# Two-layer trunk of GLA and dilated attention: the gate's columns side by side, heads two by two, another order in the first seven steps

## The chip, the cores and the metric

The kernel runs on one core of one Trainium2 chip. The metric is the device time of one execution in microseconds (us); the median of three runs stands for a kernel. TensorE (PE) multiplies, VectorE (DVE), ScalarE (ACT) and GpSimd (POOL) do the work on elements, SyncE (SP) issues most transfers.

## The reference

Batch 1, 256 positions, width 2048, two layers, all in float32:

```python
# layer 0: h = rmsnorm(x, norm_mix_g[0])
a_b, a_c, a_x, q, k, v, r, g_low = jnp.split(h @ w_in, IN_OFFSETS, axis=-1)
y_conv = a_b * causal_short_conv(a_c * a_x, conv_w)          # 1024 channels, width 3
log_a = jax.nn.log_sigmoid(g_low @ w_gate2 + b_gate) / 16.0  # g_low: rank 16, out: 512
o = gla_chunked(q, k, v, log_a)                              # 4 heads, dk 128, dv 256
o = rmsnorm(o, gla_norm_g) * jax.nn.silu(r)
x = x + concatenate([y_conv, o]) @ w_out
x = x + squared_relu_mlp(rmsnorm(x, norm_mlp_g[0]), w1, w2)  # 2048 -> 8192 -> 2048
# layer 1: 16 heads of 128; three dilated groups, ALiBi, merged by their denominators
x = x + dilated_attention(rmsnorm(x, norm_mix_g[1]), w_qkv, w_o)
x = x + squared_relu_mlp(rmsnorm(x, norm_mlp_g[1]), w1, w2)
return rmsnorm(x, final_norm_g)
```

## The kernel before

**Layout.** Activations lie transposed: 16 tiles of 128 features by 256 positions. Each product with a weight is made of three fp32r products: the weight and the activation are both split into a high and a low half (`split_high` by an ACT copy L124, `split_low` by a DVE subtraction L130; `scale_split` L203 and L204 do it for x, giving one tile xs of 512 columns, high 256 and low 256), and high x high, high x low and low x high are added up in PSUM (`three`, L133 is the line of every such product).

**Steps.** The weights come as 770 blocks of 128 x 1024, one to a step: a transfer by SP into one of four `raw` buffers, the two splits (four steps ahead), and 24 products of 256 columns (groups of kind "a", tile acc) or 12 of 512 columns (kind "b", tile accv, which gives v with positions on the partitions). Eight steps make a group; behind its last step the PSUM banks are read (`evac_...`). Step 0 to 7 give q and k of the first GLA pair. Steps 8 and 9 are the gate (kind "g", tile accg): its 16 columns filled up with zeros to 128, 48 products of 256 columns. Steps 10 to 17 give v, and from step 18 on r, the second pair, the convolution, w_out, the MLP, attention (per quad one v group and two groups of q and k), w_o and the second MLP follow.

**Sub-steps and background work.** A step has four sub-steps. In each, the main loop issues the products, in the second one also `split_low` four steps ahead and the next load, then what the group's end asks for (`g.evac`), and at its end calls `advance()`, which lets exactly one waiting generator go on by one piece:

```python
for item in bg:
    if item[1] <= clock[0]:        # due, in the order of the list
        wait = next(item[0], None)
        ...
        return
```

A generator says by `yield n` after how many sub-steps its next piece is due. Each engine executes in the order of issue, so this order is the order in every queue. In the background run: the sum of squares for the first norm (squares of tiles 0 to 11 on POOL, 12 to 15 on ACT and DVE), `norm_factor` (pss: sums over partitions, at sub-step 32; prb: the factor spread over partitions, 40; `R["b"]`, 41), the pieces that wait for `R["b"]` (`after_norm`: q, k, the gate), `gates()` (pz L367: the gate's second product; la L371 to L376: log sigmoid by Abs, Exp, Ln on ACT and one DVE piece), and `gla_pair` (pg L389: cumulative sums of la, then eight levels of scores). What starts them:

```python
spawn(first_norm(), 16)
spawn(after_norm(rest), 2)      # evac_glow; rest ends with spawn(gates(), 12)
triggers[len(steps)] = lambda pair=pair: spawn(gla_pair(pair), 6)   # behind the v group
```

`evac_v` copies each half of v from PSUM on ACT (L350) in the second and the fourth sub-step of the v group's last step.

**Attention.** `evac_aqk` writes q and k of a pair of heads on DVE and starts two generators `head(h)`, due 4 and 5 sub-steps later: bias and scores (pqk L584, L585), softmax, transposes (ppt L603), a copy (pT L606), the products with v (pao), and the split into y.

Of the kernel before, what the change touches and what calls it, by code (L numbers as in the profile page):

```python
# [49 lines left out]
def trunk_kernel(ctx: ExitStack, tc, xin, vecs, w_in, w_gate, w_gate2, w_out, w_qkv, w_o, w1, w2, w2f,  # L50
# [27 lines left out]

    gpool = tc.alloc_tile_pool(name="gla", bufs=1)
    msk = gpool.tile([P, 8, P], U8, name="msk")  # L80
    wg2 = gpool.tile([P, 512], F32, name="wg2")
    ap_ = {}

    def end_gla():

# [10 lines left out]

    busy = tmp.tile([P, T], F32, tag="sqp", bufs=1, name="busy")
    pool.memset(busy, 0.0)
    p = bank("warm")
    for _ in range(WARM):  # L100
        pe.matmul(p[:, :T], lhsT=busy[:, :P], rhs=busy, start=True, stop=True)
# [12 lines left out]

    def load(s):
        g, i = steps[s]
        raws[s] = wts.tile([P, 1024], F32, tag="raw", bufs=RAW, name=f"raw{s}")
        for c in parts(s):
            nc.sync.dma_start(raws[s][:, c], g.src[g.first + i, :, c])

    def split_high(s):
        his[s] = wts.tile([P, 1024], F32R, tag="wh", bufs=WB, name=f"wh{s}")
        for c in parts(s):
            act.activation(his[s][:, c], raws[s][:, c], AF.Copy)  # L124

    def split_low(s):
        r = raws.pop(s)
        los[s] = wts.tile([P, 1024], F32R, tag="wl", bufs=WB, name=f"wl{s}")
        for c in parts(s):
            dve.tensor_tensor(los[s][:, c], r[:, c], his[s][:, c].bitcast(F32), op=OP.subtract)  # L130
# [11 lines left out]
    def part_of(g, j):  # L142
        return g.ps[j // 2][:, (j % 2) * T:(j % 2 + 1) * T]

    def sub_a(g, i, j, wh, wl):
        if j // 2 not in g.ps:
            g.ps[j // 2] = bank(f"acc{j // 2}")
        p = part_of(g, j)
        for kk in range(2):
            n = 2 * i + kk  # L150
            c = slice(kk * 512 + j * P, kk * 512 + (j + 1) * P)

            three(p, wh[:, c], wl[:, c], g.rhs(n), n == 0 and j % 2 == 0, n == 15)
# [14 lines left out]
    def sub_g(g, i, j, wh, wl):  # L168
        if 0 not in g.ps:
            g.ps[0] = bank("accg")  # L170
        p = g.ps[0]
        for kk in range(2 * j, 2 * j + 2):
            n = 8 * i + kk
            c = slice(kk * P, (kk + 1) * P)
            three(p[:, :T], wh[:, c], wl[:, c], g.rhs(n), n == 0, n == 15)

# [137 lines left out]
        return ys[k]  # L316


    gl = {"ended": 0}

    def evac_qk(pair):
        def f(j, p):
# [28 lines left out]
        return f  # L351

    def evac_glow(j, p):
        t = grab(p, "sq", 2)
        ga = gl["ga"] = gpool.tile([32, T], F32, tag="ga", bufs=1, name="ga")
        dve.memset(ga, 1.0)

        def rest():
            dve.tensor_tensor(ga[:16, :], t[:16, :], R["b"][:16, :], op=OP.mult)
            spawn(gates(), 12)  # L360
        spawn(after_norm(rest), 2)

    def gates():
        la = gl["la"] = gpool.tile([P, 2, 512], F32, tag="la", bufs=1, name="la")
        ps = [bank("pz") for _ in range(2)]
        for tt in range(2):
            pe.matmul(ps[tt], lhsT=gl["ga"][:17, tt * P:(tt + 1) * P], rhs=wg2[:17, :],  # L367
                      start=True, stop=True)
        yield 3
        for tt in range(2):  # L370
            act.activation(la[:, tt, :], ps[tt], AF.Abs)  # L371
        act.activation(la, la, AF.Exp, scale=-1.0)
        act.activation(la, la, AF.Ln, bias=1.0)
        yield 1
        for tt in range(2):
            dve.scalar_tensor_tensor(la[:, tt, :], ps[tt], 0.0, la[:, tt, :], op0=OP.min,  # L376
                                     op1=OP.subtract)
        yield 1
# [186 lines left out]
    def evac_aqk(pair):  # L565
        def f(j, p):
            if j == 0:
                at["q", pair] = ap_["p"].tile([P, 2, T], F32, tag="gq", name="aq")
                at["k", pair] = ap_["p"].tile([P, 2, T], F32, tag="gk", name="ak")
            dst = at["q" if j < 2 else "k", pair][:, j % 2, :]  # L570
            dve.tensor_tensor(dst, p, R["b"], op=OP.mult)
            if j == 3:
                (spawn(head(2 * pair), 4), spawn(head(2 * pair + 1), 5))
        return f

    def head(h):
        q, k = at["q", h // 2][:, h % 2, :], at["k", h // 2][:, h % 2, :]
        v = at["v"][h // 4]
        vc = slice((h % 4) * DH, (h % 4 + 1) * DH)
        slope = 2.0 ** (-8.0 * (h + 1) / HEADS)  # L580
        bias = ap_["p"].tile([P, 384], F32, tag="bias", name="bias")
        dve.scalar_tensor_tensor(bias, ap_["dl"][:, 0, :], slope, ap_["dl"][:, 1, :], op0=OP.mult, op1=OP.add)
        ps = bank("pqk")
        pe.matmul(ps[:, :P], lhsT=q[:, :P], rhs=k[:, :P], start=True, stop=True)  # L584
        pe.matmul(ps[:, P:384], lhsT=q[:, P:], rhs=k, start=True, stop=True)  # L585
        yield 1
        st = ap_["p"].tile([P, 3, P], F32, tag="st", name="st")
        sf = st.rearrange("p b t -> p (b t)")
        dve.scalar_tensor_tensor(sf, ps[:, :384], DH ** -0.5, bias, op0=OP.mult, op1=OP.add)
        nm = ap_["p"].tile([P, 3], F32, tag="nm", name="nm")  # L590
        dve.tensor_reduce(nm, st, axis=AX.X, op=OP.max, negate=True)
        dve.tensor_tensor(nm[:, 1:2], nm[:, 1:2], nm[:, 2:3], op=OP.min)
        z = ap_["p"].tile([P, 2], F32, tag="z", name="z")
        act.activation(sf[:, :P], sf[:, :P], AF.Exp, bias=nm[:, 0:1], accum_out=z[:, 0:1])
        act.activation(sf[:, P:], sf[:, P:], AF.Exp, bias=nm[:, 1:2], accum_out=z[:, 1:2])
        yield 2
        dve.reciprocal(z, z)
        dve.tensor_scalar(sf[:, :P], sf[:, :P], z[:, 0:1], None, op0=OP.mult)
        dve.tensor_scalar(sf[:, P:], sf[:, P:], z[:, 1:2], None, op0=OP.mult)
        yield 9  # L600
        pt = bank("ppt")
        for b in range(3):
            pe.transpose(pt[:, b * P:(b + 1) * P], st[:, b, :], ident)  # L603
        yield 1
        pT = ap_["p"].tile([P, 384], F32, tag="pT", name="pT")
        act.activation(pT, pt[:, :384], AF.Copy)  # L606
        yield 3
        po = bank("pao")
        mm(po[:, :T], v[:, 0, vc], pT[:, :T], True, False)
        mm(po[:, P:T], v[:, 1, vc], pT[:, T:], False, True)  # L610
        yield 1
        y = y_tile(h)
        split_into(y, po[:, :T])
        yield 1


    hs = {}
# [40 lines left out]
    for pair in range(2):  # L658
        add(Group(w_in, 32 * pair, 8, "a", X, evac_qk(pair)))
        if pair == 0:  # L660
            add(Group(w_gate, 0, 2, "g", X, evac_glow))
        add(Group(w_in, 32 * pair + 8, 8, "b", X, evac_v(gl["v"], pair)))
        triggers[len(steps)] = lambda pair=pair: spawn(gla_pair(pair), 6)
        if pair == 0:
            add(Group(w_in, 16, 8, "a", X, evac_r(0)))
            add(Group(w_in, 24, 8, "a", X, evac_r(1)))
# [34 lines left out]
        load_x(s + 4)  # L701
        load(s + RAW)
    act.dma_start(cm, cmat)
    act.dma_start(wg2[:17, :], w_gate2)

    def first_norm():
        for k in range(12, NK):
# [13 lines left out]
            yield 8  # L721
    spawn(load_masks(), 40)

    SUB = {"a": (sub_a, 4), "b": (sub_b, 4), "g": (sub_g, 4)}
    for s, (g, i) in enumerate(steps):
        if s in triggers:
            flush()
            triggers[s]()
        if s < 4:
            first_scale(s + 4)  # L730
        if s + LA < len(steps):
            split_high(s + LA)
        f, n = SUB[g.kind]
        wh, wl = his.pop(s), los.pop(s)
        for j in range(n):
            f(g, i, j, wh, wl)
            if j == 1:
                if s + LA < len(steps):
                    split_low(s + LA)
                if s + LA + RAW < len(steps):  # L740
                    load(s + LA + RAW)
            flush()
            if i == g.n - 1:
                if g.kind == "a" and j % 2 == 1:
                    g.evac(j - 1, part_of(g, j - 1))
                    g.evac(j, part_of(g, j))
                    del g.ps[j // 2]
                elif g.kind == "b" and j % 2 == 1:
                    g.evac(j // 2, g.ps.pop(j // 2))
                elif g.kind == "g" and j == n - 1:  # L750
                    g.evac(0, g.ps.pop(0)[:, :T])
            advance()
    flush()
    while bg:
# [38 lines left out]
def _layout(x, norm_mix_g, norm_mlp_g, final_norm_g, hyb_w_in, conv_w, gla_w_gate2, gla_b_gate,  # L793
# [16 lines left out]
        c = slice(h * 512, h * 512 + 512)  # L810
        parts += [ac[:, c], ax[:, c], ab[:, c]]
    a["w_in"] = _blocks(np.concatenate(parts, axis=1))
    gp = np.zeros((2, P, 8, P), np.float32)
    gp[..., :16] = g.reshape(2, 8, P, 16).transpose(0, 2, 1, 3)
    a["w_gate"] = gp.reshape(2, P, 1024)
    a["w_gate2"] = np.concatenate([f(gla_w_gate2[0]), f(gla_b_gate[0])[None]], axis=0)
    wo = f(hyb_w_out[0]).reshape(NK, P, D)
    a["w_out"] = _blocks(wo[[0, 1, 2, 3, 8, 9, 10, 11, 12, 13, 14, 15, 4, 5, 6, 7]].reshape(D, D))
# [36 lines left out]
```

## Time and profile before

| | |
|---|---|
| median of three runs | 2186.46 us (2186.12 to 2186.83) |
| the profiled execution | 2186.37 us, its span 2184.2 us |
| PE, PEld (weight load) busy | 2168.6 us, 2137.3 us |
| DVE, ACT, POOL busy | 1323.4, 1038.8, 66.9 us |
| HBM read | 406.94 MB, 187 GB/s over the span |
| chain that ended last | PE 98%, DVE 1%, DMA 1% |

Matmuls are pipelined, and a busy PE is not PE at its peak. A product of 256 columns has a record of 276 ns, and the next one starts 0.11 us after it. The chain of waits is followed back from the last instruction, at each step to what released it.

### The profile page before, as it was taken

The numbers are of one execution on the slowest core, as the hardware profiler recorded it, in microseconds if no ns is written. First come the engines' busy times: TensorE is split into PE (matmuls) and PEld (weight loads), VectorE is DVE, ScalarE is ACT, GpSimd is POOL, SyncE is SP. The second block draws the span as 40 slices with busy tenths as digits, with TensorE's granted clock in tenths as the row PEclk, the third lists the DMA queues.
The fourth block names the chain that finished last, engine by engine and source line by source line (L and its number), as shares of the span: only waits on it lengthen the run. The fifth ranks groups of instructions, "written<-read, shape, count | busy, mean of one in ns | idle before, by whom it ended". The sixth has DMA issues, their size and how long they took to land.

```text
span 2184.2 us, 43375 instructions
## 1 busy us (share of the span) xinstructions
PE 2168.6 (99%) x18390; PEld 2137.3 (98%) x18390; DVE 1323.4 (61%) x1809; ACT 1038.8 (48%) x1414; POOL 66.9 (3%) x70
## 2 busy tenths in 40 slices
PE   9999999999999999999999999999999999999997
PEld 8999999999999999999999999999999999999997
DVE  7666766655556555656665655666555555555555
ACT  5555545444444354345444444545434534444553
POOL 4000230000000000000000000000000000000000
PEclk9999999999999999999999999999999999999999
DMA  7555566656666656665665555565666565666663
GB/s 264 159 171 166 163 201 186 196 190 208 186 199 189 202 184 203 190 198 183 205 191 169 177 176 174 173 195 186 199 194 194 189 198 191 197 195 195 191 199 117
DMA packets 114405, 411.86 MB, mean 189 GB/s; under 512 B 12817, under 2 KB 13201, under 8 KB 114210
## 3 DMA queue, kind: packets, MB, share of 16 engines
q1 hardware_dynamic: 113760, 408.47, 59.3%
q8 instruction: 144, 2.36, 0.4%
q10 hardware_dynamic: 450, 0.61, 0.1%
q14 instruction: 51, 0.42, 0.1%
HBM read 406.94 MB, written 2.10 MB: 187 GB/s over the span
## 4 chain that ended last, share of the span: by engine, by line
PE 98%; DVE 1%; DMA 1%; issue 0%; ACT 0%; SPq 0%; DVEq 0%; ACTq 0%
PE acc L133 88%; PE accv L133 6%; PE accg L133 1%; PE psc L450 1%; DMA raw<-w_in 1%; PE pao L133 0%; DVE wl L130 0%; PE pqk L585 0%; PE po L133 0%; PE ppt L603 0%; DVE xs L204 0%; DVE xf L761 0%; PE pqk L584 0%; PE pos L133 0%; PE pss L133 0%
## 5 line engine op out<-in xcount | busy, mean ns | idle before, releaser
L130 DVE TENSOR_TENSOR wl<-raw,wh 128x1024 fp32r<-128x1024 f32 (+1 forms) x771 | 936.7, 1229 | 708.0 <-ACT wh L124 707.3
L124 ACT ACTIVATE wh<-raw 128x1024 fp32r<-128x1024 f32 (+1 forms) x771 | 810.3, 1058 | 851.7 <-PE acc L133 739.5
L133 PE MATMUL acc<-xs,wh 128*128 128x256 f32 x6400 | 1100.8, 277 | 0.1
L133 PEld LDWEIGHTS acc<-xs,wh 128*128 128x128 f32 x6400 | 966.0, 188 | 1.7 <-ACT wh L124 0.8
L133 PE MATMUL acc<-xs,wl 128*128 128x256 f32 x3200 | 885.1, 277 | 2.2 <-DVE wl L130 2.2
L133 PE MATMUL acc<-hs,wh 128*128 128x256 f32 x3968 | 675.0, 276 | 0.0
L133 PEld LDWEIGHTS acc<-xs,wl 128*128 128x128 f32 x3200 | 600.9, 188 | 3.9 <-DVE wl L130 3.9
L133 PEld LDWEIGHTS acc<-hs,wh 128*128 128x128 f32 x3968 | 597.2, 188 | 0.0
L133 PE MATMUL acc<-hs,wl 128*128 128x256 f32 x1984 | 547.6, 276 | 0.0
L133 PEld LDWEIGHTS acc<-hs,wl 128*128 128x128 f32 x1984 | 372.4, 188 | 0.0
L133 PE MATMUL acc<-ys,wh 128*128 128x256 f32 x1024 | 175.3, 277 | 0.0
L133 PEld LDWEIGHTS acc<-ys,wh 128*128 128x128 f32 x1024 | 154.4, 188 | 0.1
L133 PE MATMUL acc<-ys,wl 128*128 128x256 f32 x512 | 141.4, 276 | 0.0
L133 PE MATMUL accv<-wh,xs 128*128 128x512 f32 x384 | 122.1, 399 | 0.0
L276 DVE TENSOR_TENSOR hs<-u,hs 128x256 fp32r<-128x256 f32 x128 | 54.5, 426 | 79.0 <-ACT hs L275 79.0
L133 PEld LDWEIGHTS acc<-ys,wl 128*128 128x128 f32 x512 | 96.1, 188 | 0.0
L275 ACT ACTIVATE hs<-u 128x256 fp32r<-128x256 f32 x128 | 53.4, 417 | 71.1 <-DVE u L627 71.1
L133 PEld LDWEIGHTS accv<-wh,xs 128*128 128x128 f32 x384 | 70.2, 188 | 14.3 <-issue 0.8
L133 PE MATMUL accv<-wl,xs 128*128 128x512 f32 x192 | 75.5, 393 | 0.0
L289 DVE TENSOR_TENSOR x<-x,t 128x256 f32<-128x256 f32 x128 | 54.4, 425 | 4.4
L627 DVE TENSOR_TENSOR u<-u 128x256 f32<-128x256 f32 x128 | 53.5, 418 | 0.0
L287 DVE TENSOR_TENSOR t<-acc,rb 128x256 f32<-128x256 f32 x124 | 51.8, 417 | 0.0
(148 smaller groups left out, 790.5 us busy)
## 6 DMA issues: line engine op xcount, KB each, us to landing
raw<-w SPq DMA_DIRECT2D x504, 512.0 KB, 4.3
raw<-w_qkv SPq DMA_DIRECT2D x96, 512.0 KB, 3.6
raw<-w_in SPq DMA_DIRECT2D x95, 512.0 KB, 3.7
raw<-w_out SPq DMA_DIRECT2D x32, 512.0 KB, 4.2
raw<-w_o SPq DMA_DIRECT2D x32, 512.0 KB, 4.3
raw<-w2f SPq DMA_DIRECT2D x8, 512.0 KB, 4.3
x<-xin SPq DMA_DIRECT2D x8, 256.0 KB, 5.9
out_dram<-xf SPq DMA_DIRECT2D x7, 256.0 KB, 2.3
```

The source lines that it names most:

```text
L124: act.activation(his[s][:, c], raws[s][:, c], AF.Copy)
L130: dve.tensor_tensor(los[s][:, c], r[:, c], his[s][:, c].bitcast(F32), op=OP.subtract)
L133: pe.matmul(out_, lhsT=lhsT, rhs=rhs, start=start, stop=stop, skip_group_check=True)
L275: act.activation(t[:, :T], v, AF.Copy)
L276: dve.tensor_tensor(t[:, T:], v, t[:, :T].bitcast(F32), op=OP.subtract)
L287: dve.tensor_tensor(t, p, R["b2"], op=OP.mult)
L289: dve.tensor_tensor(x[:, k, :], x[:, k, :], p, op=OP.add)
L450: pe.matmul(p[:, (2 * h + tt) * P:(2 * h + tt + 1) * P], lhsT=l[:, h, c], rhs=r[:, h, c], start=True, stop=True)
L627: dve.tensor_tensor(u, u, u, op=OP.mult)
```

## The change

Three edits. (1) In steps 0 to 6 `sub_a` calls `early`, which issues the products of the high weights for all four column blocks in the first two sub-steps and those of the low weights in the last two. (2) The gate becomes one step of kind "h": its weights come as one block of 128 x 256; ACT copies the high halves into columns 0 to 15 and DVE the low halves into columns 32 to 47 of four tiles wg3, which POOL has set to zero at the start. 16 products of 512 columns (xs high and low side by side) follow; `evac_glow` adds the two halves of the high rows, and the low rows stay apart until the second product, for which wg2 holds the gate's second matrix twice (49 rows, the last one the bias). (3) One generator `heads(pair)` does two heads at a time.

```diff
+    pool.memset(wg2[:32, :], 0.0)
+    wg3 = [const.tile([P, 4, P], F32R, tag=f"ys{4 + i}", name=f"wg3{i}") for i in range(4)]
+    for t in wg3:
+        pool.memset(t.bitcast(F32), 0.0)
...
     def split_high(s):
+        if steps[s][0].kind == "h":
+            r = raws[s][:, :256].rearrange("p (k c) -> p k c", c=16)
+            for q in range(4):
+                act.activation(wg3[q][:, :, :16], r[:, 4 * q:4 * q + 4, :], AF.Copy)
+            his[s] = None
+            return
...
     def split_low(s):
         r = raws.pop(s)
+        if steps[s][0].kind == "h":
+            r = r[:, :256].rearrange("p (k c) -> p k c", c=16)
+            for q in range(4):
+                dve.tensor_tensor(wg3[q][:, :, 32:48], r[:, 4 * q:4 * q + 4, :],
+                                  wg3[q][:, :, :16].bitcast(F32), op=OP.subtract)
...
+    def early(g, i, j, wh, wl):
+        if j < 3:
+            todo = [(1, jj) for jj in ((0, 1), (2, 3), ())[j]] + [(0, jj) for jj in ((), (), (0, 1))[j]]
+        else:
+            todo = [(0, 2), (0, 3)]
+        for high, jj in todo:
+            p = part_of(g, jj)
+            for kk in range(2):
+                n = 2 * i + kk
+                c = slice(kk * 512 + jj * P, kk * 512 + (jj + 1) * P)
+                hi, lo = g.rhs(n)[:, :T], g.rhs(n)[:, T:]
+                if high:
+                    mm(p, wh[:, c], hi, n == 0 and jj % 2 == 0, False)
+                    mm(p, wh[:, c], lo, False, False)
+                else:
+                    mm(p, wl[:, c], hi, False, n == 15)
...
+        if s_now[0] < 7:
+            early(g, i, j, wh, wl)
+            return
...
+    def sub_h(g, i, j, wh, wl):
+        if 0 not in g.ps:
+            g.ps[0] = bank("accg")
+        for n in range(4 * j, 4 * j + 4):
+            mm(g.ps[0], wg3[n // 4][:, n % 4, :], g.rhs(n), n == 0, n == 15)
...
     def evac_glow(j, p):
-        t = grab(p, "sq", 2)
-        ga = gl["ga"] = gpool.tile([32, T], F32, tag="ga", bufs=1, name="ga")
+        t = tmp.tile([P, T], F32, tag="sq", name="gt")
+        act.activation(t[:64, :], p[:64, :T], AF.Copy)
+        dve.tensor_tensor(t[:16, :], t[:16, :], p[:16, T:], op=OP.add)
+        ga = gl["ga"] = gpool.tile([64, T], F32, tag="ga", bufs=1, name="ga")
         dve.memset(ga, 1.0)
         def rest():
             dve.tensor_tensor(ga[:16, :], t[:16, :], R["b"][:16, :], op=OP.mult)
+            dve.tensor_tensor(ga[32:48, :], t[32:48, :], R["b"][32:48, :], op=OP.mult)
             spawn(gates(), 12)
...
-            pe.matmul(ps[tt], lhsT=gl["ga"][:17, tt * P:(tt + 1) * P], rhs=wg2[:17, :],
+            pe.matmul(ps[tt], lhsT=gl["ga"][:49, tt * P:(tt + 1) * P], rhs=wg2[:49, :],
...
-                (spawn(head(2 * pair), 4), spawn(head(2 * pair + 1), 5))
+                spawn(heads(pair), 4)
...
+    def heads(pair):
+        for h in hp:
+            pe.matmul(ps[h][:, :P], lhsT=q[:, :P], rhs=k[:, :P], start=True, stop=True)
+            pe.matmul(ps[h][:, P:384], lhsT=q[:, P:], rhs=k, start=True, stop=True)
+        for h in hp:
...
+            yield 1        # bias | scores, max, exp
...
+            yield 2
+        for h in hp:       # reciprocal, two scalings
...
+            yield 1
+        yield 7
+        for h in hp:
+            pt[h] = bank("ppt")
+            for b in range(3):
+                pe.transpose(pt[h][:, b * P:(b + 1) * P], st[h][:, b, :], ident)
+        yield 1
+        for h in hp:
+            act.activation(pT[h], pt[h][:, :384], AF.Copy)
+        yield 4
+        po = bank("pao")   # both heads in one bank
...
+        yield 1
+        for h in hp:
+            split_into(y_tile(h), po[:, (h % 2) * T:(h % 2 + 1) * T])
+            yield 1
...
-            add(Group(w_gate, 0, 2, "g", X, evac_glow))
+            add(Group(w_gate, 0, 1, "h", X, evac_glow))
...
-    act.dma_start(wg2[:17, :], w_gate2)
+    act.dma_start(wg2[:16, :], w_gate2[:16, :])
+    act.dma_start(wg2[32:49, :], w_gate2)
...
-    a["w_gate"] = gp.reshape(2, P, 1024)
+    a["w_gate"] = np.ascontiguousarray(g.reshape(NK, P, 16).transpose(1, 0, 2)).reshape(P, 256)
```

## Rows read from the trace of the kernel before

**Rows 1.** Windows, 33.77 to 2171 us: length, busy time (count) by engine, PEclk, DMA
```profile
33.77:2171.00 2137.23, 2137.09 (x18178) 2109.46 (x18178) 1288.70 (x1762) 1016.91 (x1377) 44.51 (x42) 1.00 0.60 188
```

**Rows 2.** Chain that ended last, 24 to 75 us: start us, us, what
```profile
27.46 1.64 DVE xs L204 x2
...
33.29 0.43 DVE ssq L218
...
33.77 1.05 PE pss L133 x8
34.82 5.55 PE accg L133 x48
40.37 0.44 PE prb L256 x4
40.81 17.17 PE accv L133 x75
...
59.89 5.02 PE accv L133 x21
64.91 4.11 PE acc L133 x36
69.02 0.89 PE pg L389 x8
```

**Rows 3.** Timeline of PE: start us, us, line, operation, out<-in, count, idle time before
```profile
27.52 0.38 PE L133 MATMUL acc<-xs,wl 128*128 128x256 f32 x1 [0.29 <-DVE wl L130]
...
30.36 0.32 PE L133 MATMUL acc<-xs,wl 128*128 128x256 f32 x1
...
32.80 0.28 PE L133 MATMUL acc<-xs,wl 128*128 128x256 f32 x1
...
61.77 0.39 PE L133 MATMUL accv<-wl,xs 128*128 128x512 f32 x1
```

**Rows 4.** Chain, the stretch of the first MLP and an attention group
```profile
415.46 680.70 PE acc L133 x6006
...
1387.58 6.82 PE acc L133 x60
```

**Rows 5.** Timeline of DVE
```profile
29.02 2.35 DVE L130 TENSOR_TENSOR wl<-raw,wh 128x1024 fp32r<-128x1024 f32 x2
...
65.31 1.29 DVE L376 SCALAR_TENSOR_TENSOR la<-pz,la 128x512 f32<-128x512 f32 x2 [5.89 <-ACT la L373]
```

**Rows 6.** Groups by line and form: count | busy us, mean ns | idle before us
```profile
L124 ACT ACTIVATE wh<-raw 128x1024 fp32r<-128x1024 f32 x769 | 809.1, 1059 | 851.7 <-PE acc L133 739.5 <-issue 74.9 <-PE accv L133 24.8
...
L606 ACT ACTIVATE pT<-ppt 128x384 f32<-128x384 f32 x16 | 7.7, 482 | 1.0 <-PE ppt L603 0.5
...
L427 ACT ACTIVATE E<-G,gs 128x64 f32<-128x64 f32 x4 | 1.4, 344 | 0.0
...
L98 POOL MEMSET busy<- 128x256 f32 x1 | 0.3, 311 | 0.3 <-POOLq L845 0.3
L396 DVE TENSOR_TENSOR gs<-G 128x2 f32<-128x2 f32 x2 | 0.3, 154 | 0.0
```

**Rows 7.** Timeline of ACT from the gate's second product on
```profile
59.93 0.60 ACT L371 ACTIVATE la<-pz 128x512 f32<-128x512 f32 x1 [0.26 <-PE pz L367]
...
65.18 1.05 ACT L124 ACTIVATE wh<-raw 128x1024 fp32r<-128x1024 f32 x1
66.13 1.24 ACT L350 ACTIVATE v<-accv,rc 128x512 f32<-128x512 f32 x2
```

**Rows 8.** Windows at the end, columns as in rows 1
```profile
2174.80:2175.40 0.60, 0.60 (x4) 0.46 (x3) 0.00 (x0) 0.00 (x0) 0.00 (x0) 0.50 0.00 0
```

**Rows 9.** Chain at the end
```profile
2167.91 2.85 PE accg L133 x25
...
2174.53 1.03 PE prb L256 x4
```

**Rows 10.** Timeline of PE at the start
```profile
1.09 4.63 PE L101 MATMUL warm<-busy 128*128 128x256 f32 x10 [1.09 <-POOL busy L98]
```

More of the change, by code (lines that the diff above doesn't have):

```diff
@@ L80, in trunk_kernel @@
     msk = gpool.tile([P, 8, P], U8, name="msk")
-    wg2 = gpool.tile([P, 512], F32, name="wg2")
-    ap_ = {}
+    wg2 = gpool.tile([64, 512], F32, name="wg2")
+    ap_, gl = {}, {"ended": 0}
     def end_gla():
@@ L116, in load @@
         g, i = steps[s]
+        if g.kind == "h":
+            raws[s] = wts.tile([P, 1024], F32, tag="raw", bufs=RAW, name=f"raw{s}")
+            nc.sync.dma_start(raws[s][:, :256], g.src)
+            return
         raws[s] = wts.tile([P, 1024], F32, tag="raw", bufs=RAW, name=f"raw{s}")
@@ L127, in split_low @@
         r = raws.pop(s)
+        if steps[s][0].kind == "h":
[3 more added lines that the diff above has]
+                                  wg3[q][:, :, :16].bitcast(F32), op=OP.subtract)
+            los[s] = None
+            return
         los[s] = wts.tile([P, 1024], F32R, tag="wl", bufs=WB, name=f"wl{s}")
@@ L143, in part_of @@
         return g.ps[j // 2][:, (j % 2) * T:(j % 2 + 1) * T]
+    s_now = [0]
+    def early(g, i, j, wh, wl):
[14 more added lines that the diff above has]
+                    mm(p, wl[:, c], hi, False, n == 15)
     def sub_a(g, i, j, wh, wl):
+        if i == 0 and j == 0:
+            g.ps = {jj: bank(f"acc{jj}") for jj in range(2)}
         if j // 2 not in g.ps:
@@ L148, in sub_a @@
         p = part_of(g, j)
+        if s_now[0] < 7:
+            early(g, i, j, wh, wl)
+            return
         for kk in range(2):
@@ L316, in y_tile @@
         return ys[k]
-    gl = {"ended": 0}
     def evac_qk(pair):
@@ L572, in f @@
             if j == 3:
-                (spawn(head(2 * pair), 4), spawn(head(2 * pair + 1), 5))
+                spawn(heads(pair), 4)
         return f
[L576 to L585, printed above, removed]
-        yield 1
[L587 to L603, printed above, removed]
-        yield 1
[L605 to L614, printed above, removed]
@@ new lines, in heads @@
+    def heads(pair):
+        hp = (2 * pair, 2 * pair + 1)
+        v = at["v"][pair // 2]
+        ps, st, z, pt, pT = {}, {}, {}, {}, {}
+        for h in hp:
+            q, k = at["q", pair][:, h % 2, :], at["k", pair][:, h % 2, :]
+            ps[h] = bank("pqk")
+            pe.matmul(ps[h][:, :P], lhsT=q[:, :P], rhs=k[:, :P], start=True, stop=True)
+            pe.matmul(ps[h][:, P:384], lhsT=q[:, P:], rhs=k, start=True, stop=True)
+        for h in hp:
+            slope = 2.0 ** (-8.0 * (h + 1) / HEADS)
+            bias = ap_["p"].tile([P, 384], F32, tag="bias", name="bias")
+            dve.scalar_tensor_tensor(bias, ap_["dl"][:, 0, :], slope, ap_["dl"][:, 1, :],
+                                     op0=OP.mult, op1=OP.add)
+            yield 1
+            s_ = st[h] = ap_["p"].tile([P, 3, P], F32, tag="st", name="st")
+            sf = s_.rearrange("p b t -> p (b t)")
+            dve.scalar_tensor_tensor(sf, ps[h][:, :384], DH ** -0.5, bias, op0=OP.mult, op1=OP.add)
+            nm = ap_["p"].tile([P, 3], F32, tag="nm", name="nm")
+            dve.tensor_reduce(nm, s_, axis=AX.X, op=OP.max, negate=True)
+            dve.tensor_tensor(nm[:, 1:2], nm[:, 1:2], nm[:, 2:3], op=OP.min)
+            zz = z[h] = ap_["p"].tile([P, 2], F32, tag="z", name="z")
+            act.activation(sf[:, :P], sf[:, :P], AF.Exp, bias=nm[:, 0:1], accum_out=zz[:, 0:1])
+            act.activation(sf[:, P:], sf[:, P:], AF.Exp, bias=nm[:, 1:2], accum_out=zz[:, 1:2])
+            yield 2
+        for h in hp:
+            sf = st[h].rearrange("p b t -> p (b t)")
+            dve.reciprocal(z[h], z[h])
+            dve.tensor_scalar(sf[:, :P], sf[:, :P], z[h][:, 0:1], None, op0=OP.mult)
+            dve.tensor_scalar(sf[:, P:], sf[:, P:], z[h][:, 1:2], None, op0=OP.mult)
+            yield 1
[4 more added lines that the diff above has]
+                pe.transpose(pt[h][:, b * P:(b + 1) * P], st[h][:, b, :], ident)
+        yield 1
+        for h in hp:
+            pT[h] = ap_["p"].tile([P, 384], F32, tag="pT", name="pT")
+            act.activation(pT[h], pt[h][:, :384], AF.Copy)
+        yield 4
+        po = bank("pao")
+        for h in hp:
+            vc = slice((h % 4) * DH, (h % 4 + 1) * DH)
+            o_ = po[:, (h % 2) * T:(h % 2 + 1) * T]
+            mm(o_, v[:, 0, vc], pT[h][:, :T], h % 2 == 0, False)
+            mm(o_[:, P:], v[:, 1, vc], pT[h][:, T:], False, True)
+        yield 1
+        for h in hp:
+            split_into(y_tile(h), po[:, (h % 2) * T:(h % 2 + 1) * T])
+            yield 1
@@ L722, in trunk_kernel @@
     spawn(load_masks(), 40)
-    SUB = {"a": (sub_a, 4), "b": (sub_b, 4), "g": (sub_g, 4)}
+    SUB = {"a": (sub_a, 4), "b": (sub_b, 4), "g": (sub_g, 4), "h": (sub_h, 4)}
     for s, (g, i) in enumerate(steps):
+        s_now[0] = s
         if s in triggers:
@@ L751, in trunk_kernel @@
                     g.evac(0, g.ps.pop(0)[:, :T])
+                elif g.kind == "h" and j == n - 1:
+                    g.evac(0, g.ps.pop(0))
             advance()
@@ L812, in _layout @@
     a["w_in"] = _blocks(np.concatenate(parts, axis=1))
-    gp = np.zeros((2, P, 8, P), np.float32)
-    gp[..., :16] = g.reshape(2, 8, P, 16).transpose(0, 2, 1, 3)
-    a["w_gate"] = gp.reshape(2, P, 1024)
+    a["w_gate"] = np.ascontiguousarray(g.reshape(NK, P, 16).transpose(1, 0, 2)).reshape(P, 256)
     a["w_gate2"] = np.concatenate([f(gla_w_gate2[0]), f(gla_b_gate[0])[None]], axis=0)
```

## The prediction

> **What bounds the kernel now.** I read the windows first, then the chain of waits, then the timelines of the engines around the places where the chain leaves TensorE (PE). The window from 33.77 to 2171 us shows PE busy for 2137.09 of 2137.23 us at the full clock [rows 1]: from there on the time is the sum of what PE executes, and only three things can change it: less PE work, an earlier beginning of that window, or a new wait of PE inside it. The chain up to 33.77 us runs over VectorE (DVE), not PE [rows 2]: the low halves of x and of the weights (xs L204, wl L130) follow one another, and PE stands waiting for them once in a step, 0.29 us in the row shown, in six steps alike [rows 3]. The execution profiled took 2186.37 us, of which the span is 2184.2; the median of the three runs is 2186.46, so sums made on the profile move over with 0.1 us added.
>
> **High products first in steps 0 to 6.** Nothing is added or removed: 24 products a step, the 8 low ones last. So a step can begin before its wl is there, and after wl only 8 products remain. Take step 6: its wl is there at 27.46, where DVE turns to the next xs [rows 2]; now one low product follows at 27.52 and then most of the step; after the change 16 products are done by then, 8 remain at 0.1133 us each (680.70 us for 6006 [rows 4]), and the step ends near 28.4 instead of 30.1. But step 7 keeps the old order: its third product needs wl7, the first of two DVE pieces that begin at 29.02 and take 2.35 together, done near 30.2 [rows 5]. Before, that product came at 30.36 [rows 3]; it comes at 30.3 now. The lead won in six steps is lost in the seventh, because DVE, not PE, is the chain. Behind step 7 PE waits again: the last product starts at 32.80 [rows 3], and pss waits until DVE has added the last square at 33.29 plus 0.43 [rows 2]. What brings pss forward is DVE's own queue: the gate's low split there is the second of the two pieces at 29.02, 1.17 us [rows 5], and becomes four pieces of 64 columns, each between 0.15 us (two columns [rows 6]) and 0.3, about 0.8 together. That gives 0.35 us; the most is 0.75, until PE's own step 7 holds pss (32.80 plus 0.28). In the other direction there are five memsets on POOL at the start, at most 0.62 each by twice the row for 256 columns [rows 6], which end near 4 us instead of 1; POOL's sum of squares is wanted 30 us later, so I allow 0.3 us of loss. Term: -0.35 (bounds -0.75 and +0.3).
>
> **The gate.** 48 products of 256 columns, 5.55 us, become 16 of 512 columns. The same form stands next to it: 75 of them in 17.17 us, 0.229 each [rows 2], so 3.66 us, and -1.89. Its poorest price, 21 in 5.02 us behind pz, would give 3.82 and -1.73. SyncE's (SP's) queue loads 128 KB once where it loaded 512 KB twice, at the same place; ACT's queue has one issue more. On ACT four copies of 64 columns at 0.344 replace two splits of 1.06 [rows 6]. The evacuation adds a DVE addition that waits for an ACT copy; behind it stands the low split for a step four later, which is 11 us of PE work away, so it costs nothing. pz has 49 rows instead of 17 and the same columns: no change.
>
> **What the gate's shorter step moves.** This is the term that matters. The background work is timed in sub-steps (four to a step, one `advance` each). R["b"] is set at sub-step 41, one after prb, and the gate's rest, 12 later gates(), follow from that; the chain agrees, since 75 products of v, three to a sub-step, lie between prb and pz [rows 2], 40 + 25 = 65. So pz stays behind sub-step 65 and the ScalarE (ACT) pieces of la behind sub-step 68. The gate has 4 sub-steps fewer, so the v group that follows ends at sub-step 68 instead of 72, and gla_pair, hung on its end, issues pg at 74 instead of 78. Two things follow.
> First, between pz and pg there are now 9 sub-steps instead of 13: by the chain, pg at 69.02 less 12 products of 0.229 is 66.27, on the old time axis [rows 2].
> Second, both copies of v (L350) are issued at sub-steps 66 and 68, each ahead of its `advance`, so in ACT's queue they now stand ahead of la; before they came behind it, at 66.13 [rows 7]. ACT executes in order. The second copy needs the last product of sub-step 68, which on that axis starts at 61.77 and ends 0.39 later [rows 3], so it begins near 62.2; then 0.62 for it (two in 1.24), 0.55 for the first Abs, and the second Abs starts near 63.35 instead of 59.93 [rows 7], 3.4 later. Everything behind it is a fixed chain: to the end of la on DVE, 65.31 plus 1.29 [rows 5], it is 6.67 us, so la is there at 70.0. pg asks for it at 66.27. PE stands still 3.75 us; one of its head pairs may begin on the first half of la, so I take +3.65 (the least +0.35, if the copies of v do not delay la and only the 9 sub-steps count, 66.60 against 66.27; the most +4.0). Behind pg on PE is the whole of the r group, so nothing hides it. DVE waits in the same time at L376 with the low split of step 21 behind it, wanted four steps later.
>
> **Attention two by two.** The same instructions: 16 heads with their products, transposes and copies. What goes is half of the changes between kinds of product: 60 products behind a transposed or attention piece take 6.82 us, 0.02 more than 60 at 0.1133 [rows 4]. Six such returns a pair become three, 8 pairs: 24 times 0.02, -0.5 (bounds 0 and -0.6). The second head's pqk moves up next to the first, and its keys are ready by then, since they are written right after the first head's. The last write of y comes one sub-step earlier than now, so w_o does not wait.
>
> **Sum.** -0.35 - 1.89 - 0.5 + 3.65 = +0.9: 2187.3 by the profile, 2187.4 by the median. Its own range, from the sizes of the four terms, is 2186.8 to 2188.0.
>
> **Rivals.**
> *The clock falls in the new wait: slower.* At the end of the kernel PE's clock falls to 0.50, the level of 1.2 GHz [rows 8], after the last dense products ended at 2170.8 [rows 9]; the four products of prb then take 1.03 us [rows 9] instead of 0.44 [rows 2]. Here a pause of 3.7 us with a fragment of pg inside would resemble that; against it, no wait of the trace ends in dense work at the low level. The price: at the start ten passes of 256 columns take 4.63 us [rows 10], 0.46 each, about double two 128-column passes of prb at full clock, so work at half pace lasts for some microseconds before it rises. Between 0 and 3 us are lost, 1.5 in the middle: 2188.9, at the most 2190.4. It decides if the clock has fallen when pg begins.
> The Trainium skill, page "TensorE: Matmul & The Clock Gate", section "HAM oscillation — how this bites in real kernels", speaks for this rival: a wait between bursts of matmuls brings the throttle back and the next burst starts slow. By that rule the forecast moves to this rival's time; the end of the trace agrees that idleness lowers the clock (0.50), and no run yet shows it for a single pause.
> *No new wait.* If la is ready for pg after all, say because ACT gets to la before the copies of v, only 0.35 of the 3.65 is left: 2184.1. For it: the order within ACT's queue is read from the code, not from a row. Against: before, the order of la, the next high split and v in the trace is exactly the code's [rows 7].
> *A wait in attention.* Both heads' pT copies (0.48 each [rows 6]) now stand before both of the pair's output products, with 4 sub-steps, 2.7 us, to do so, beside a high split of 1.06. If ACT is over 0.7 us late, PE waits for the rest, in each of 8 pairs: at 0.5 each 4 us, 2191.4. ACT is busy for 1016.91 of 2137.23 us [rows 1], so I think little of it.
> *The high products do more than I think:* the lead of step 6 reaches pss, 0.4 more, 2187.0; this is within the forecast's range.
>
> **How the numbers follow.** Forecast 0.6, clock 0.2, no new wait 0.12, attention 0.05, anything else 0.03. About 0.2% (4.4 us) is what a measurement of this kernel can tell from no change. Under 2182.1 only the case without the wait could come, with over 1 us more gain than its bounds show: 0.05. Over 2190.8 come the clock's dearest outcomes (0.04), attention (0.03) and others: 0.09. Range 2183.8 to 2190.2: from the case without a wait to the clock's upper end.
>
> **What would show it.** After: accg as 16 products in about 3.7 us; pss near 33.4; pz some 2.2 us earlier than now; ACT's order v, v, Abs, Abs; a wait of PE at pg (L389's counterpart) on DVE's la of 3 to 4 us; products at 0.114 right behind it (or at twice that, if the clock fell); three returns a pair in attention and no PE wait there. I am wrong if pg does not wait, if PE gains more than 0.75 us ahead of accg, or if another wait of PE over 0.5 us appears between accg and 2160 us.

## The result and the profile after: 34.6 us slower, of which 31 behind attention

The kernel after takes 2220.89 us (median of 4 runs, 2219.53 to 2221.86), the one before, on the same chip, 2186.29 (2185.89 to 2186.83): 1.0157 times as long, 95% interval 1.0145 to 1.0169. The forecast, 2187.4 with a range up to 2190.2, was wrong. The execution profiled took 2219.53 us with a span of 2217.7, against 2184.2.

The first view is again the windows, of after. The columns are those of [rows 1].

```profile
32.66:2204.60 2171.94, 2168.73 (x18146) 2140.51 (x18146) 1288.70 (x1763) 1017.01 (x1376) 44.58 (x42) 1.00 0.58 184
1500.00:2100.00 600.00, 600.00 (x5097) 600.00 (x5096) 336.90 (x429) 263.17 (x333) 0.00 (x0) 1.00 0.59 185
```

The same stretch of the second MLP before:

```profile
1500.00:2100.00 600.00, 600.00 (x5297) 600.00 (x5296) 348.49 (x441) 271.51 (x343) 0.00 (x0) 1.00 0.62 194
```

From pss to the last product PE is idle for 3.21 us in all (2171.94 less 2168.73). In 600 us of the second MLP it is busy for 600 in both kernels, at the full clock in both, and yet it does 5097 products instead of 5297. The busy share and the clock row say nothing here: the count in the window does. The chain of waits shows where it begins. After (start us, us, what):

```profile
417.52 680.70 PE acc L155 x6006
...
1146.24 10.60 PE acc L155 x90
1156.84 0.66 PE ppt L669 x6
1157.50 3.42 PE acc L155 x30
1160.92 1.31 PE pao L155 x8
1162.22 6.36 PE acc L155 x54
...
1406.05 84.80 PE acc L155 x720
...
1491.19 5.55 PE acc L155 x48
1496.74 0.44 PE prb L310 x4
1497.19 684.76 PE acc L155 x5814
2181.95 22.63 PE accg L155 x192
```

And before, for the parts that have no row yet:

```profile
1403.24 80.26 PE acc L133 x708
...
1483.84 5.76 PE acc L133 x48
1489.60 0.44 PE prb L256 x4
1490.04 658.94 PE acc L133 x5814
2148.98 21.78 PE accg L133 x192
```

Divide each row's time by its count. The first MLP has 113.3 ns a product in both kernels ([rows 4] and 680.70 for 6006). The second has 113.3 before (658.94 for 5814) and 117.8 after (684.76 for 5814). Apart from 0.02 to 0.1 us for the change of kind at the start of a row, nothing lies between: 90 products behind pqk take 117.8, the 30 behind ppt about 114, the 54 behind pao 117.8, the 720 of w_o 117.8. So the same products run at full clock in one of two rhythms, quick (340.0 ns for the three products of a term, 680.70 / 2002) and slow (353.3), and the rhythm changes only where a short group of other products breaks the stream. Before has the slow rhythm too: the 48 products between pss and prb take 5.76 us there, 120 ns each with the change of kind in front, and 5.55 after. In both kernels pss turns the rhythm and prb turns it back, so the second MLP gets the rhythm that w_o had, and w_o gets that which the last pao left.

The timeline of PE shows it in the first rows of two terms that follow one another, after first, then before (start us, us, line, operation, out<-in, count):

```profile
1499.85 0.40 PE L155 MATMUL acc<-xs,wh 128*128 128x256 f32 x2
...
1500.20 0.40 PE L155 MATMUL acc<-xs,wh 128*128 128x256 f32 x2
```

```profile
1500.10 0.39 PE L133 MATMUL acc<-xs,wh 128*128 128x256 f32 x2
...
1500.44 0.39 PE L133 MATMUL acc<-xs,wh 128*128 128x256 f32 x2
```

Durations barely differ, since products overlap; the starts do: 0.35 us from one term to the next against 0.34.

The rest of the change, from the chain near the start, against [rows 2]:

```profile
32.66 1.05 PE pss L155 x8
33.71 3.78 PE accg L155 x16
37.49 2.77 PE accv L155 x12
...
69.39 2.15 PE pg L446 x8
71.54 5.88 PE acc L155 x48
77.42 0.89 PE psc L507 x8
```

Before, pg is followed by these:

```profile
69.91 5.46 PE acc L133 x48
75.36 0.89 PE psc L450 x8
```

PE's waits between 33 and 2170 us (in total, times, the longest); then ACT in that place, against [rows 7], and PE's clock behind the wait (windows):

```profile
PE pg L446 <- DVE la L433: 3.2, 1, 3.2
```

```profile
60.73 0.69 ACT L403 ACTIVATE v<-accv,rc 128x512 f32<-128x512 f32 x1 [2.68 <-PE accv L155]
62.12 0.69 ACT L403 ACTIVATE v<-accv,rc 128x512 f32<-128x512 f32 x1 [0.69 <-PE accv L155]
62.70 1.08 ACT L428 ACTIVATE la<-pz 128x512 f32<-128x512 f32 x2
```

```profile
68.00:72.50 4.50, 3.11 (x15) 3.10 (x16) 3.55 (x4) 3.01 (x4) 0.00 (x0) 0.62 0.16 15
72.50:76.00 3.50, 3.50 (x33) 3.50 (x32) 1.59 (x3) 1.06 (x1) 0.00 (x0) 1.00 0.77 279
```

Both copies of v stand ahead of la, pg waits 3.21 us, and the clock falls with it: mean 0.62 in the first window, whose first 1.4 us are still the wait, and 1.00 behind it. The whole, from the starts of the same pieces in the two chains:

| up to the start of | before | after | after minus before | this stretch |
|---|---|---|---|---|
| pss | 33.77 | 32.66 | -1.11 | -1.11 |
| v, behind the gate | 40.37 (prb) | 37.49 | -2.88 | -1.77 |
| pg | 69.02 | 69.39 | +0.37 | +3.25 |
| psc behind it | 75.36 | 77.42 | +2.06 | +1.69 |
| first MLP | 415.46 | 417.52 | +2.06 | 0 |
| w_o | 1403.24 | 1406.05 | +2.81 | +0.75 |
| end of the products | 2170.76 | 2204.58 | +33.82 | +31.01 |
| end of the span | 2184.2 | 2217.7 | +33.5 | -0.3 |

The +31.01 are 6726 products (720 of w_o, 5814 and 192 of the second MLP) at 4.44 ns more each, 29.9, and the 12 products by which w_o's row is longer than before, 1.36 at 0.113, since the last pao stands two sub-steps earlier in the stream (the row above lacks them), less 0.2 for the 48 products behind pss.

### The profile page after: what moved, and what is told of

It reads as the page before. It is cut to its first block, busy times and chain, and to the rows that moved or that the text cites. A ratio compares the mean times of both kernels' runs of the same rounds, so it can differ in the third digit from the quotient of the medians.

```text
span 2217.7 us, 43336 instructions
## 1 busy us (share of the span) xinstructions
PE 2199.1 (99%) x18358; PEld 2167.6 (98%) x18358; DVE 1323.4 (60%) x1813; ACT 1038.6 (47%) x1416; POOL 69.5 (3%) x75
## 4 chain that ended last, share of the span: by engine, by line
PE 98%; DVE 1%; issue 0%; DMA 0%; ACT 0%; SPq 0%; DVEq 0%; ACTq 0%
PE acc L155 88%; PE accv L155 6%; PE accg L155 1%; PE psc L507 1%; PE pao L155 0%; DVE xs L258 0%; PE pqk L642 0%; DVE wl L152 0%; DMA raw<-w_in 0%; PE po L155 0%; PE ppt L669 0%; DVE xf L835 0%; PE pqk L641 0%; PE pos L155 0%; PE pg L446 0%
## 5 line engine op out<-in xcount | busy, mean ns | idle before, releaser
L155 PE MATMUL acc<-hs,wh 128*128 128x256 f32 x3968 | 687.7, 278 | 0.0
L155 PEld LDWEIGHTS acc<-hs,wh 128*128 128x128 f32 x3968 | 604.6, 189 | 0.0
```

The lines of the kernel that those rows point to most:

```text
L155: pe.matmul(out_, lhsT=lhsT, rhs=rhs, start=start, stop=stop, skip_group_check=True)
```

## The experiments

The theory ("rhythm"): pairing the heads makes groups of other products of another length, the last of these leaves TensorE in the slow rhythm, and nothing in w_o and the second MLP turns it for good. The rival ("gate"): the gate's missing step shifts which weight block lies in which buffer, and the slower products come from there.

**The heads alone.** The kernel before with the heads in pairs:

```
-                (spawn(head(2 * pair), 4), spawn(head(2 * pair + 1), 5))
+                spawn(heads(pair), 4)
```

> The kernel before with the paired heads as the only edit. Theory R (the paired breaks of attention leave TensorE in a slower rhythm, 117.8 instead of 113.3 ns for a product of 256 columns, which lasts until another break): +30 to +32 us, 2216 to 2218; the second MLP at 117.8. Theory G (the gate's missing step shifts which weight and PSUM buffers meet, and that makes the products slower): the heads alone bring -0.5 us, 2185.8, and 113.3 throughout.

Measured 2218.07 (before 2186.45; ratio 1.0145, 1.0130 to 1.0161). The pairs alone cost 31.6 us, with the gate and its steps as before.

**All but the heads.** The kernel after with the old `head(h)` and the line above taken back:

> The changed kernel with the heads of the kernel before. Theory R: the slow rhythm is gone; what is left is the start (-1.1), the gate (-1.8) and the wait at pg with its 3.4 us at half clock (+4.9), together +2.0: 2188.3. Theory G: the slow rhythm stays, 2218 to 2221.

Measured 2189.24 (1.0013, 1.0004 to 1.0023). Its second MLP:

```profile
1493.21 658.94 PE acc L155 x5814
```

The gate rival is out, from both sides: 658.94 us with the gate's step missing, 684.76 with it there (the run before this one).

**Output products one sub-step apart.** The pairs stay; only the 8 passes of pao become 4 and 4 (each of these products in plain float32 has two records in the trace, its passes):

```
             mm(o_[:, P:], v[:, 1, vc], pT[h][:, T:], False, True)
-        yield 1
+            yield 1
```

> The changed kernel, only the two heads' products with v (pao) one sub-step apart, four passes each as before. If the rhythm behind a break is set by how many passes stand together in it, the 720 products of w_o behind the last pao run at 113.3 instead of 117.8 ns, and by the turn at each later norm so does the second MLP: 30 us less than the changed kernel, near 2190. If the whole of the pairing or anything else of attention's order sets it, nothing changes: 2220.

Measured 2190.62 (1.0020, 1.0010 to 1.0031). One `yield`, moved into its loop, brings 30 us back:

```profile
1405.25 0.65 PE pao L155 x4
1405.91 0.70 PE acc L155 x6
1406.61 0.65 PE pao L155 x4
1407.26 80.94 PE acc L155 x714
```

714 products at 113.4 ns. Neither half turned the rhythm: the six products between them take 0.70 us, and from the second on their starts lie 120, 117, 116 and 114 ns apart in the packed trace, like those behind the second half (120, 116, 116, 114) and unlike those behind the eight passes of after (118, 117, 119, 117). So eight passes in one group turned it here, four and four did not. In the kernel before, the four passes of the second head too leave the quick rhythm as it is: in the last pair the 36 products ahead of them take 113.9 ns each, the 708 behind them 113.4. Those of the first head meet six slow products, 118 ns from start to start, and end the slow stretch, so four passes can turn it in another place.

```profile
1398.49 4.10 PE acc L133 x36
1402.59 0.65 PE pao L133 x4
```

**Two spare products, in both kernels.** If the rhythm is a state of TensorE alone, products that no other engine uses should turn it too. Two products of 128 columns into unused columns of prb's bank, two sub-steps behind the prb that stands ahead of the second MLP, read by nothing:

```
+        R["n"] += 1
+        if R["n"] == 4:
+            for tt in range(2):
+                pe.matmul(p[:, T + tt * P:T + (tt + 1) * P], lhsT=c[:, tt:tt + 1].to_broadcast([P, P]),
+                          rhs=ident, start=True, stop=True)
+            yield 1
```

> The kernel before with two spare products (four passes of 128 columns into unused columns of a PSUM bank that nobody reads) two sub-steps behind prb of the norm ahead of the second MLP. Theory R (a state of TensorE alone, turned by an extra break): the 5800 products behind it run at 117.8 ns, +26 us, 2212. If the slow rhythm needs what attention's heads do on VectorE and ScalarE, or another use of buffers: +0.5 us, 2186.8.

> The changed kernel with the same two spare products behind prb of the norm ahead of the second MLP. Theory R: there the changed kernel is in the slow rhythm, and the extra break turns it to the fast one, so the 5800 products behind it return to 113.3 ns: -26 us, 2195. Rival (any extra break makes what follows slow, or the slowness belongs to the paired heads' buffers): no change or slower, 2221 or more.

Measured: before with it 2213.73 (1.0125, 1.0104 to 1.0145), after with it 2194.91 (1.0039, 1.0025 to 1.0054). The same 0.44 us of work makes the one kernel 27 us slower and the other 26 us faster. First before, then after, each with the spare pair:

```profile
1491.99 0.44 PE prb L270 x4
1492.43 683.35 PE acc L133 x5802
```

```profile
1499.70 0.44 PE prb L324 x4
1500.15 657.58 PE acc L155 x5802
```

**The wait at pg.** The kernel of the second experiment with the gate's second product, which the spawn sets off, four sub-steps earlier:

```
-            spawn(gates(), 12)
+            spawn(gates(), 8)
```

> The changed kernel with the heads of before and the gate's second product called 8 instead of 12 sub-steps behind its rest, so that la stands ahead of both copies of v in ScalarE's queue and 13 sub-steps lie between pz and pg again. If the wait at pg and the half clock behind it (3.2 + 1.7 us) come from that order, both go and the gate's and the start's gain are left: 2189.2 - 4.9 = 2184.3, about 2 us under the kernel before. If the wait has another cause: 2189.

Measured 2183.94 (ratio 0.9988, 0.9979 to 0.9997), 5.3 less than without it. PE has no wait left between 34 and 2160 us; la stands ahead of v on ACT, and pg takes 0.89 us again:

```profile
57.01 0.60 ACT L428 ACTIVATE la<-pz 128x512 f32<-128x512 f32 x1 [0.86 <-PE pz L424]
...
64.06 1.25 ACT L403 ACTIVATE v<-accv,rc 128x512 f32<-128x512 f32 x2
```

So wait and half clock came from the gate's second product being called too late behind the shorter gate. The edit gives back two things at once, la's place ahead of v on ACT and the 13 sub-steps between pz and pg; this run does not part them. It beats both kernels, by 2.6 us against before: small, but the interval leaves out 1.

**High products first, alone.** The kernel before with only that part:

> The kernel before with only the high products first in steps 0 to 6. My step says that the lead is lost in step 7, whose third product waits for wl7: 0 to -0.1 us, 2186.4. If the lead reaches pss: -0.7 us, 2185.8.

Measured 2186.54 (1.0000, 0.9991 to 1.0009). The profile of one execution adds something: in step 7 PE waits 1.86 us for wl, and then goes through that step at a mean clock of 0.52 (windows).

```profile
30.08 0.39 PE L133 MATMUL acc<-xs,wl 128*128 128x256 f32 x1 [1.86 <-DVE wl L130]
```

```profile
30.30:33.80 3.50, 3.50 (x19) 3.50 (x19) 3.40 (x6) 1.56 (x3) 0.00 (x0) 0.52 0.69 228
```

The lead of six steps is turned into one wait. In the kernel after the same wait is 1.32 us, with the clock staying at 1.00.

**Which break turns the rhythm.** Thirty spare breaks in the first MLP of the kernel before, 24 sub-steps apart: products of 128 columns (1, 1, 2, 2, 3, 3, 4, 4, 5, 5, 6, 6, 8, 8 of them), products of 256 (1, 1, 2, 2), transposes (1, 1, 2, 2, 3, 3, 6, 6), pqk of one head (twice) and of two (twice):

> The kernel before with 30 short breaks in the first MLP, 24 sub-steps apart, of spare products that nobody reads: 1 to 8 products of 128 columns (two passes each), 1 and 2 of 256 columns, 1 to 6 transposes, and 1 and 2 heads' worth of pqk. Theory R: the rate of the 144 products between breaks takes only two values, 113.3 and 117.8 ns, and which breaks turn it is seen from the sequence; from the traces so far, 2 and 3 products of 128 columns turn it, 4 of them do not, one head's pqk does not and two heads' do. Rival (the rate follows from what stands in the buffers, not from breaks): 113.3 throughout. Time: 15 us of spare work and up to 15 us of slow rhythm, 2200 to 2216.

Measured 2217.28, above what was expected. Only the two rates occur, constant between breaks. Of the rules quoted above, put together from the first traces, only that for two products held. For 128-column products another showed: an even number turned it each time, an odd one never. Of the other kinds some turned it once and not the next time. Two more runs asked for these. The first has 50 groups of 128-column products at changing distances, in the order of this list (number, distance in sub-steps, times):

```
BREAKS = [("m", n, gap) for n, gap, m in ((2, 24, 8), (2, 7, 6), (2, 13, 6), (2, 25, 4), (1, 24, 4), (1, 7, 4),
                                          (1, 13, 4), (3, 24, 3), (3, 13, 3), (4, 13, 8)) for _ in range(m)]
```

> The kernel before with 50 spare breaks in the first MLP, all of products of 128 columns: groups of 2 products (24, 7, 13 and 25 sub-steps apart; 24 groups), of 1 (12), of 3 (6) and of 4 (8). Theory 'number' (as the first run with spare breaks had it: an even number of 128-column products turns the rhythm every time, an odd number never): all 32 even groups turn, none of the 18 odd ones; the rhythm is slow in 258 sub-steps of 6 products, 6.9 us at 4.44 ns; with 110 products at 0.22 and 50 returns at 0.02 the time is 2186.5 + 24.2 + 1.0 + 6.9 = 2218.6, and the second MLP is untouched. Rival 'place' (the place in the stream decides, so the distance to the last break matters): some groups of 2 don't turn or some of 1 or 3 do, most likely where the distance changes; the time may lie anywhere between 2211.7 and 2240.

Measured 2218.48, against 2218.6. All 32 even groups turned the rhythm, none of the 18 odd ones did. The odd groups of both runs all met the quick rhythm; what they do in the slow one was not tried. Groups of four, 78 products apart:

```profile
1001.21 0.89 PE spare L93 x8
1002.10 8.86 PE acc L151 x78
1010.96 0.89 PE spare L93 x8
1011.85 9.19 PE acc L151 x78
```

The number of products is not the whole rule even for this kind. The kernel's own pg is four products of 128 columns as well, 8 passes in 0.89 us, and so is psc in the rows above. At full clock the rhythm behind pg is quick, 48 products in 5.46 us, and the 48 behind each psc of four products take 5.46 us too. The spare products multiply the identity by itself, those of pg and psc have other operands; which difference counts was not tried.

The second has 60 groups of the other kinds:

> The kernel before with 60 spare breaks in the first MLP: one product of 256 columns (18 times, at 24, 13 and 7 sub-steps), two of them (18 times, the same distances), 1, 2 and 3 transposes (6 times each, 13 apart) and one head's two pqk products (6 times, 13 apart). In the first run with spare breaks the same group turned the rhythm once and not the next time for each of these kinds. Theory 'history' (the group and the rhythm that it meets decide, not the distance): within a kind each group that meets the slow rhythm does the same, and each that meets the fast one does the same, whatever the distance. Rival 'place': the outcomes change with the distance. Time by either: 2186.5 + about 33 for the spare products, + up to 22 for slow stretches: 2220 to 2242.

Measured 2230.92. Both theories fell. Single products of 256 columns went through a cycle of four, the same at all three distances: the first turns the quick rhythm into the slow one, the next two leave it slow, and the fourth brings the quick one back.

```profile
493.28 16.96 PE acc L152 x144
...
510.67 16.96 PE acc L152 x144
...
528.06 16.96 PE acc L152 x144
...
545.46 16.33 PE acc L152 x144
```

So distance is not it, and neither are the group and the rhythm that it meets. Of the 18 pairs of such products, the second brought the quick rhythm back and the 16 behind it left it so. Three transposes turned it each time in this run, but only once of twice in the first; one head's pqk turned it each time in both, yet in attention before it leaves it quick (the 60 products behind it take 6.82 us [rows 4]); one or two transposes showed no order that I can name. What breaks are counted by stays open.

**The whole change with both orders mended.** Output products apart and the gate's second product at 8:

> The whole change with two orders mended: the two heads' output products one sub-step apart (short break, 4 and 4 passes) and the gate's second product spawned 8 sub-steps after its trigger instead of 12. If the two costs are separate, this is the time of the change with output products apart (2190.6) less what the earlier gate gave the kernel with the old heads (2189.2 - 2183.9 = 5.3): 2185.3, not faster than the same with the heads one by one (2183.9). If the earlier gate shifts the breaks against each other, the second MLP may turn slow again: 2212 or more.

Measured 2185.78 (0.9996, 0.9986 to 1.0005), 0.5 above the sum of the two, so the costs are separate. With the heads one by one the kernel is 1.8 us quicker still.

## Why the prediction was wrong

**The step that failed** is "Attention two by two": "What goes is half of the changes between kinds of product", -0.5, with bounds of 0 and -0.6. The step priced a break by what it costs where it stands. That part came true: up to w_o the pairs cost +0.75, with 12 products fewer in the stretch (1.36), so +2.1; 621 products in the slow rhythm ahead of the last pao (90 behind pqk and 63 or 72 behind pao, in four of the eight pairs) make +2.8 at 4.44 ns, which leaves some -0.6 for the returns saved, by difference. What a break costs behind it, the rhythm that it leaves, was in no term and no bound. It was worth +29.9 us: a single moved `yield` took it away, and so did two spare products for the second MLP. A row that would have raised the question was in the trace before: the 48 products between pss and prb at 5.76 us, beside 5.46 for the same 48 behind pg. That "only three things can change it: less PE work, an earlier beginning of that window, or a new wait of PE inside it" was thus wrong: the pace of the same work is a fourth.

**The wait at pg** came as worked out, la behind both copies of v on ACT: 3.21 us against 3.65. The rival that the clock falls in it came true too: pg took 2.15 instead of 0.89 and the 48 products behind it 5.88 instead of 5.46, +1.7, against the 1.5 put on it. The Trainium skill ("TensorE: Matmul & The Clock Gate", section "HAM oscillation — how this bites in real kernels") has a wait between bursts bring the throttle back; this single wait agrees, at a mean clock of 0.62 from 68 to 72.5 us. I gave it 0.2 and the case without it 0.6, on no row of a single pause.

**The gate**: -1.77, against -1.89. **The start**: -1.11 in this profile against -0.35, but where x lands differs between runs, so the better number is that of the other profiles: pss begins at 33.28 to 33.46 in the five with the new gate (mean 33.34), and at 33.77 to 34.18 in the six with the old gate and the old order (33.96): -0.62, within its bounds (by the rows named for it, 33.77 less 33.08, the most to gain was 0.69 and not 0.75). The four low splits of the gate together take 0.62 us where one took 1.17, a little less than the 0.8 supposed. That the lead of the first six steps is lost in step 7 was right. **No wait in attention**: right.

Without the pairs the change takes 2189.2 (second experiment), 1.8 above the forecast and within the range: the clock's part.

## What to carry to other kernels

Where one engine is busy all the time, compare the start-to-start interval of the same instruction in the same stage, before and after: its busy share and its clock did not show a 4% slower stream here, and the durations hardly did. An edit of a few short instructions can decide the pace of thousands behind it, so a change in a long stream's interruptions is priced with that as a case of its own, and tried by moving or adding one interruption. When an early step is shortened, work set off by counts of steps moves against work set off by data; look at each in-order queue for what now stands ahead of the urgent piece.

## What the runs showed of the hardware

TensorE ran back-to-back fp32r products of 256 columns at full clock at 113.3 or 117.8 ns, and nothing between, over at least 6006 products without a change. Groups of an even number of spare 128-column products turned it in 40 cases of 40, of an odd number, all in the quick rhythm, in none of 24; pg and psc, four products of 128 columns with other operands, left it quick, so the number alone does not decide. For wider products, transposes and mixed groups no rule was found. It repeats from run to run: the four runs of after lie within 2.3 us. What in the engine it is was not tried. A wait of 1.86 us was seen with a fall of the clock to 0.52 behind it, and one of 1.85 us in step 7 of the run with the output products apart with 1.00 from 30.3 to 33.8 us: the wait's length alone does not tell it.
